# Softmaxes, rotated heads and latents transposed whole in float32 and parted out of PSUM

## The chip, the cores and the metric

The kernel runs on one core of a Trainium2 chip. The metric is the device time of one execution in microseconds; the kernel before takes 2120.96 us (median of 3 runs, 2120.81 to 2120.97). Engine names in the rows are those of the profile: PE is TensorE (PEld its loading of the array), DVE VectorE, ACT ScalarE, SP the queue that issues DMAs.

## The reference

A two-layer encoder over 256 tokens of 2048 features, in float32. Each layer has a token mixer and a channel mixer, each as `x = x + RMSNorm(f(RMSNorm(x)))`:

```
layer 0 mixer: proj = h @ w_in                       # 2048 -> 4608
   A: 8 heads of 128, rotary q and k, dilated windows (as a mask of log counts on full scores)
   B: 8 query heads on 2 key/value heads, RMSNorm of each head's q and k, two-dimensional rotary
   out = [A | B] @ w_out
layer 1 mixer: c = h @ w_in                          # 512 query latents, 512 key/value latents, 64 rotary key
   q = norm(c_q) @ w_uq, k, v = norm(c_kv) @ w_ukv   # 16 heads, 128 + 64 rotary
   out = attention @ w_out
attention: softmax(q k^T * scale) v, 256 x 256 scores for each head
channel mixer: (gelu(conv3(h @ w_gate)) * (h @ w_val)) @ w_down     # 5632 wide
```

## The kernel before, in words

Float32 accuracy comes from splitting: each operand of a product is kept as two float32r tiles, a high part (the value rounded to float32r) and a low part (the value less the high part), and a product is the sum of high times high, high times low and low times high. `parted` (L521) makes them: ScalarE copies the high part, VectorE subtracts it from the value. `parted_by` does it for a value times a row's factor.

Weights stream in chunks of 128 x 1024 (four raw buffers). `_split` parts each, up to two chunks ahead of the products (three buffers of `whi`, `wlo`; L117 on ScalarE, L118 on VectorE). A chunk in `proj_tok` feeds 12 products of 512 columns (L172 to L174), in the channel mixer's `proj_t` 16 products (L186, L187), in layer 1's small projections 24 of 256 columns.

Between chunks, `tick` advances generators by a step each: evacuations of projections (`turned`, `latent`, `evac_qr`, `evac_kr`) and heads (`attend`). The tile framework then orders the instructions of an engine; what is marked to stay in program order (scores and transposes) keeps its place in its own sequence. So attention work lies in between the products of the next projection.

A head in `attend`: scores of two query blocks into one PSUM bank (L471), the maxima on VectorE (L480 or L478), exponentials with row sums on ScalarE (L487) into `p`, the reciprocal (L489). Then `phl`, the two parts of p / sum (L492, L493). Three ticks later each part is turned by four transposes of 128 x 128 (L252, `turn`, against the identity in float32r `ident_r`), eight in all, through two PSUM banks, and ScalarE copies the banks into `pT` (L506). Two ticks later come the products with the values (L172 to L174 `pT,v`) and the parts of the result (L518, L519). `use["phl"]` bounds how many heads hold parts at a time: 1 in layer 0, 2 in layer 1.

`turned` (L538) applies the rotary embedding to up to four heads with the tokens on the partitions (`y`, `z` on VectorE), parts the result into `hl` and turns both parts of each head, four transposes and one ScalarE copy (L574) a head. `latent` in layer 1 does the same for the four 128-wide blocks of a latent (L768). The rotary queries and the shared rotary key of layer 1 (L833, L816) also go through `hl` and `turn`.

PSUM has four banks under the tag `acc` for projections and four under `at` for scores, transposes and attention results. At the seams between sublayers the residual x is transposed in plain float32 against `ident` (L413).

Of the kernel before, what the change touches and what calls it, by code (L numbers as in the profile page):

```python
# [16 lines left out]
P = 128  # L17
T = 256
# [8 lines left out]
HOLD = 3        # chunks of weights kept at the end of an output projection, see proj_tok  # L27
LAGS = 3, 2, 1  # ticks from a softmax to its transposes, from these to the values, from a rotary to its transposes

# columns of the packed vectors  # L30
# [7 lines left out]
class Model:  # L38
    """All products are of operands in two float32r parts, high and low: high high + high low + low high.

    A sublayer's input x is kept as parts of x times the pre-norm's gain, features on the partitions; the norm's
    factor of a token goes in where the products leave PSUM (or into the factors of the scores).
    """
# [14 lines left out]
    def now(self, gen, after=()):  # L58
        """A generator that steps at every tick, once those of `after` have ended."""
        self.soon.append((gen, tuple(after)))  # L60
        return gen

    def later(self, gen, after=()):
        """A generator of the queue, of which a few run at a time."""
        self.bg.append((gen, tuple(after)))
        return gen
# [55 lines left out]
    def behind(self, instructions):  # L122
        """A block whose instructions are issued after these, on their engines."""
        stack = ExitStack()
        for ins in instructions:
            stack.enter_context(self.tc.issue_after(ins.ins))
        return stack

    def weights(self, upto=None):
        """The parts of the next chunk; those after it, before `upto`, get split and loaded."""  # L130
        i = self.at
        if upto is None:
            upto = i + (2 if self.lead else 3)
            self.follow()
        for j in range(i, upto):
            self._split(j)
        for j in range(upto, i + 6):
            self._load(j) if j < upto + 4 else None
        self.at += 1
        return self.made.pop(i)  # L140

    def follow(self):
        """Ahead of a chunk: the tiles of x that it meets, if they aren't there yet."""
# [7 lines left out]
    def warm(self, n):  # L151
        """Products of zeros, for the array's clock to stay up while its next operands get made."""
# [5 lines left out]
    def acc(self, n):  # L158
        """n PSUM banks for sums; evacuations that would still hold them come first."""
# [9 lines left out]
    def mm3(self, ps, lh, ll, rh, rl, start, stop):  # L169
        """ps (+)= l.T @ r of operands in two parts."""  # L170
# [5 lines left out]
    def proj_t(self, nk, x, tag):  # L176
        """[512 outputs] x [256 tokens], outputs on the partitions: 4 PSUM tiles, their halves to be added."""
# [13 lines left out]
    def proj_tok(self, nk, x, order=None, before={}, hold=0):  # L191
        """[256 tokens] x [512 outputs], tokens on the partitions: 2 PSUM tiles.

        The last `hold` chunks are kept for the first half of the tokens to be done before the second.
        """
# [27 lines left out]
    def proj_small(self, x, n, nk):  # L223
        """[256 tokens] x [n outputs] of one chunk of weights [128, nk * n], tokens on the partitions."""
# [12 lines left out]
    def proj_pair(self, x):  # L237
        """Two heads of [128 outputs] x [256 tokens] of one chunk, outputs on the partitions."""
# [11 lines left out]
    def turn(self, out, x):  # L250
        """out[f, t] = x[t, f] of a float32r block."""
        self.tc.keep_in_program_order(self.nc.tensor.transpose(out, x, self.ident_r))  # L252

    def joined(self, sp, out, ps):
        """The sum of a proj_t tile's halves."""
# [9 lines left out]
    def heron(self, s, v, r):  # L265
        """r = 1 / sqrt(v) from the table's root s, by a step of Heron's rule: 2 s / (s s + v)."""
# [6 lines left out]
    def rstd_over(self, ss, r, n, dim):  # L273
        """Factors of a norm of r * x, r a row's factor, from x's square sums ss [128, 2, n], times r."""
# [19 lines left out]
    def table(self, f, x):  # L294
        """Have the table of f loaded ahead of its use, once x [128, 1] is there."""
        self.nc.scalar.activation(self.spare, x, f)

    def pre_norm(self, sp=None):
        """self.r [128 tokens, 2], and on request self.rb [128, 256 tokens] alike on all partitions; a generator."""
# [29 lines left out]
    def split(self, k, src, pre):  # L329
        """Feature tile k of x, transposed, times the gain as two float32r parts."""  # L330
# [11 lines left out]
    def out_proj(self, nk, parts, post, pre, order=None, before={}):  # L342
        """x += post-norm of the output projection; then x's parts for the next product, or x to DRAM.

        The first half of the tokens ends ahead of the second, so that its part of the norm and of the sum lies
        under products; the parts of x come in pairs of feature tiles, of which the next sublayer's first chunks
        of weights ask (see follow).
        """
# [109 lines left out]
    def attend(self, scores, sc, mask, v, v_gen, put, sp):  # L458
        """scores(i): the (lhsT, rhs) of query block i; sc [128 queries, 2]: factors of the scores, or a number;
        v(j): the parts of [128 keys, 128], there once the generator in v_gen has ended; a generator."""  # L460
        nc, use = self.nc, self.use
        while use["phl"] >= self.phl_bufs:
            yield
        use["phl"] += 1
# [8 lines left out]
        p = sp.tile([P, 2, T], F32, tag="p", name="p", bufs=2)  # L473
# [16 lines left out]
        phl = sp.tile([P, 2, 2, T], F32R, tag="phl", name="phl", bufs=self.phl_bufs)  # L490
        for i in range(2):
            nc.scalar.activation(phl[:, 0, i, :], p[:, i, :], AF.Copy, scale=den[:, i:i + 1])  # L492
            nc.vector.scalar_tensor_tensor(out=phl[:, 1, i, :], in0=p[:, i, :], scalar=den[:, i:i + 1],  # L493
                                           in1=phl[:, 0, i, :].bitcast(F32), op0=ALU.mult, op1=ALU.subtract)
# [6 lines left out]
        for a in range(2):  # L501
            pt = self.psum("at", F32R).rearrange("p (j q) -> p j q", j=2)
            for j in range(2):
                for i in range(2):
                    self.turn(pt[:, j, i * P:(i + 1) * P], phl[:, a, i, j * P:(j + 1) * P])
            nc.scalar.copy(pT[:, a], pt.bitcast(F32))  # L506
        use["phl"] -= 1
# [17 lines left out]
    def parted_by(self, hi, lo, x, r):  # L525
        """The parts of x * r."""
# [4 lines left out]
    def mixed(self, sp):  # L531
        """The attention's outputs in parts, feature tiles."""
# [5 lines left out]
    def turned(self, sp, ps, n, block, tab, put, scale=None):  # L538
        """Rotary of n heads, tokens on the partitions, neighbouring blocks of `block` turned against each other,
        times scale(t) of the rows or scale(t, i) of a head's; the parts, transposed, go to put(i); a generator."""  # L540
        nc = self.nc
        parts = []
        for t in range(2):
            x = ps[t][:, :n * P]
            y = sp.tile([P, 512], F32, tag="y", name="y", bufs=1)[:, :n * P]
            z = sp.tile([P, 512], F32, tag="z", name="z", bufs=1)[:, :n * P]
            hl = sp.tile([P, 2, 512], F32R, tag="hl", name="hl", bufs=2)
# [3 lines left out]
            nc.vector.tensor_tensor(out=heads(y), in0=heads(x), in1=tab[:, t, 0].broadcast_to([P, n, P]), op=ALU.mult)  # L551
            for a in range(2):
                nc.vector.tensor_tensor(out=blocks(z)[:, :, :, a, :], in0=blocks(x)[:, :, :, 1 - a, :],
                                        in1=sin[:, :, :, a, :].broadcast_to([P, n, P // block // 2, block]),
                                        op=ALU.mult)
            nc.vector.tensor_tensor(out=y, in0=y, in1=z, op=ALU.add)
            if scale is None:
                self.parted(hl[:, 0, :n * P], hl[:, 1, :n * P], y)
            elif scale.__code__.co_argcount == 1:
                self.parted_by(hl[:, 0, :n * P], hl[:, 1, :n * P], y, scale(t))  # L560
            else:
                for i in range(n):
                    s = slice(i * P, (i + 1) * P)
                    self.parted_by(hl[:, 0, s], hl[:, 1, s], y[:, s], scale(t, i))
            parts.append(hl)
# [3 lines left out]
        for i in range(n):  # L569
            pt = self.psum("at", F32R).rearrange("p (a t) -> p a t", a=2)  # L570
            for a in range(2):
                for t in range(2):
                    self.turn(pt[:, a, t * P:(t + 1) * P], parts[t][:, a, i * P:(i + 1) * P])
            nc.scalar.copy(put(i), pt.bitcast(F32))  # L574
            if i % 2:
                yield

    def first_x(self, sp):
        """The first parts of x, a pair of tiles ahead of each chunk of weights."""
# [24 lines left out]
    def mixer0(self, pre):  # L604
        nc, tc, a = self.nc, self.tc, self.a
        with tc.tile_pool(name="mix0", bufs=1) as sp:
# [7 lines left out]
            self.use, self.phl_bufs = {"phl": 0, "pT": 0}, 1  # L614
# [119 lines left out]
    def mixer1(self, pre):  # L734
        nc, tc, a = self.nc, self.tc, self.a
        with tc.tile_pool(name="mix1", bufs=1) as sp:
# [3 lines left out]
            self.use, self.phl_bufs = {"phl": 0, "pT": 0}, 2  # L740
# [6 lines left out]
            def latent(ps, row, out):  # L747
# [6 lines left out]
                parts = []  # L754
                for t in range(2):
                    y = sp.tile([P, 512], F32, tag="y", name="y", bufs=1)
                    hl = sp.tile([P, 2, 512], F32R, tag="hl", name="hl", bufs=2)
# [258 lines left out]
```

## Time and profile before

| | before |
|---|---|
| median of 3 runs | 2120.96 us |
| profiled execution, span | 2119.2 us |
| TensorE busy | 2106.1 us |
| VectorE busy | 1331.3 us |
| ScalarE busy | 1140.5 us |
| DMA | 385.99 MB, mean 182 GB/s |

The profiled execution's span runs from its first to its last instruction; what lies around it is what is between it and the median of the runs. The two token mixers take 43 to 275 us and 1083 to 1300 us of the span, with the output projections behind them; the channel mixers take most of the rest. A row that groups instructions has their count, their busy time (overlaps counted once), the mean duration of one, and the idle time of the engine just before them with what ended it. In the chain of waits a row is a piece of the path that ended last: start, length, what.

### The profile page before, as it was taken

The numbers are of one execution on the slowest core, as the hardware profiler recorded it, in microseconds if no ns is written. First come the engines' busy times: TensorE is split into PE (matmuls) and PEld (weight loads), VectorE is DVE, ScalarE is ACT, GpSimd is POOL, SyncE is SP. The second block draws the span as 40 slices with busy tenths as digits, with TensorE's granted clock in tenths as the row PEclk, the third lists the DMA queues.
The fourth block names the chain that finished last, engine by engine and source line by source line (L and its number), as shares of the span: only waits on it lengthen the run. The fifth ranks groups of instructions, "written<-read, shape, count | busy, mean of one in ns | idle before, by whom it ended". The sixth has DMA issues, their size and how long they took to land.

```text
span 2119.2 us, 29704 instructions
## 1 busy us (share of the span) xinstructions
PE 2106.1 (99%) x11317; PEld 1787.4 (84%) x11317; DVE 1331.3 (63%) x2004; ACT 1140.5 (54%) x1814; POOL 0.2 (0%) x4
## 2 busy tenths in 40 slices
PE   9999999999999999999999999999999999999998
PEld 7888878888888888888888998788888888888886
DVE  6776657767667666444466764576676766754444
ACT  6766546555555555334355765465555555543433
POOL 0000000000000000000000000000000000000000
PEclk9999999999999999999999999999999999999999
DMA  8545565666666666666655335566666666666664
GB/s 312 170 138 159 167 182 176 182 195 188 191 192 183 195 189 190 191 191 193 194 182 164 102 108 155 169 194 191 190 187 195 184 196 190 185 193 194 194 189 149
DMA packets 108718, 385.99 MB, mean 182 GB/s; under 512 B 12064, under 2 KB 12576, under 8 KB 108576
## 3 DMA queue, kind: packets, MB, share of 16 engines
q1 hardware_dynamic: 108288, 383.83, 60.1%
q8 instruction: 88, 1.44, 0.3%
q14 instruction: 54, 0.44, 0.1%
q10 hardware_dynamic: 288, 0.28, 0.0%
HBM read 381.96 MB, written 2.10 MB: 181 GB/s over the span
## 4 chain that ended last, share of the span: by engine, by line
PE 98%; DVE 1%; ACT 1%; DMA 0%; issue 0%; DVEq 0%; SPq 0%
PE ps L186 31%; PE ps L174 16%; PE ps L172 16%; PE ps L173 16%; PE ps L187 15%; PE ps L471 2%; PE ps L252 2%; DVE x L391 0%; PE ps L413 0%; DMA raw<-in_w_in 0%; ACT whi L117 0%; ACT junk L292 0%; PE ps L789 0%; DVE xhl L528 0%; PE ps L790 0%
## 5 line engine op out<-in xcount | busy, mean ns | idle before, releaser
L118 DVE TENSOR_TENSOR wlo<-raw,whi 128x1024 fp32r<-128x1024 f32 (+1 forms) x710 | 867.1, 1222 | 698.3 <-ACT whi L117 697.6
L117 ACT CAST whi<-raw 128x1024 fp32r<-128x1024 f32 (+1 forms) x710 | 743.8, 1048 | 775.9 <-PE ps L174 421.6
L186 PE MATMUL ps<-xhl,whi 128*128 128x512 f32 x2816 | 978.6, 394 | 1.0 <-DVE xhl L528 1.0
L187 PE MATMUL ps<-xhl,wlo 128*128 128x256 f32 x2816 | 779.1, 277 | 0.0
L186 PEld LDWEIGHTS ps<-xhl,whi 128*128 128x128 f32 x2816 | 527.6, 188 | 123.1 <-DVE xhl L528 2.1
L187 PEld LDWEIGHTS ps<-xhl,wlo 128*128 128x128 f32 x2816 | 528.9, 188 | 1.0 <-DVE wlo L118 0.5
L174 PE MATMUL ps<-whi,gl 128*128 128x512 f32 x704 | 280.9, 399 | 0.0
L173 PE MATMUL ps<-wlo,gh 128*128 128x512 f32 x704 | 277.4, 394 | 0.0
L172 PE MATMUL ps<-whi,gh 128*128 128x512 f32 x704 | 276.0, 392 | 0.0
L173 PEld LDWEIGHTS ps<-wlo,gh 128*128 128x128 f32 x704 | 132.2, 188 | 34.5
L172 PEld LDWEIGHTS ps<-whi,gh 128*128 128x128 f32 x704 | 132.2, 188 | 31.4
L174 PEld LDWEIGHTS ps<-whi,gl 128*128 128x128 f32 x704 | 132.2, 188 | 30.3
L172 PE MATMUL ps<-whi,xhl 128*128 128x512 f32 x352 | 138.5, 395 | 1.5 <-ACT whi L117 1.5
L173 PE MATMUL ps<-wlo,xhl 128*128 128x512 f32 x352 | 137.9, 392 | 0.0
L174 PE MATMUL ps<-whi,xhl 128*128 128x512 f32 x352 | 137.6, 392 | 0.0
L172 PE MATMUL ps<-whi,oh 128*128 128x512 f32 x256 | 101.5, 397 | 0.0
L174 PE MATMUL ps<-whi,ol 128*128 128x512 f32 x256 | 101.4, 396 | 0.0
L173 PE MATMUL ps<-wlo,oh 128*128 128x512 f32 x256 | 100.9, 394 | 0.0
L257 ACT COPY half<-ps 128x256 f32<-128x256 f32 x176 | 65.0, 369 | 45.7 <-PE ps L186 36.0
L172 PEld LDWEIGHTS ps<-whi,xhl 128*128 128x128 f32 x352 | 65.9, 188 | 15.1 <-ACT whi L117 1.7
L174 PEld LDWEIGHTS ps<-whi,xhl 128*128 128x128 f32 x352 | 66.0, 188 | 14.0
L173 PEld LDWEIGHTS ps<-wlo,xhl 128*128 128x128 f32 x352 | 66.1, 188 | 13.3 <-DVE wlo L118 0.9
(177 smaller groups left out, 1722.4 us busy)
## 6 DMA issues: line engine op xcount, KB each, us to landing
raw<-in_w_up SPq DMA_DIRECT2D x352, 512.0 KB, 4.2
raw<-in_w_down SPq DMA_DIRECT2D x176, 512.0 KB, 4.2
raw<-in_w_in SPq DMA_DIRECT2D x88, 512.0 KB, 4.0
raw<-in_w_out SPq DMA_DIRECT2D x64, 512.0 KB, 4.0
gb<-in_post SPq DMA_DIRECT2D x16, 256.0 KB, 4.2
raw<-in_w_qn SPq DMA_DIRECT2D x8, 512.0 KB, 3.6
raw<-in_w_kn SPq DMA_DIRECT2D x8, 512.0 KB, 3.5
raw<-in_w_v SPq DMA_DIRECT2D x8, 512.0 KB, 3.6
```

The lines of the kernel that those rows point to most:

```text
L117: self.nc.scalar.copy(hi[:, s], raw[:, s])
L118: self.nc.vector.tensor_tensor(out=lo[:, s], in0=raw[:, s], in1=hi[:, s].bitcast(F32), op=ALU.subtract)
L172: mm(ps, lh, rh, start=start, stop=False)
L173: mm(ps, lh, rl, start=False, stop=False)
L174: mm(ps, ll, rh, start=False, stop=stop)
L186: mm(out[i], hi[:, s], x(k), start=k == 0, stop=False)
L187: mm(out[i][:, :T], lo[:, s], x(k)[:, :T], start=False, stop=k == nk - 1)
L252: self.tc.keep_in_program_order(self.nc.tensor.transpose(out, x, self.ident_r))
L257: self.nc.scalar.copy(b, ps[:, T:])
L471: nc.tensor.matmul(ps[:, i, :], l, r, start=n == 0, stop=n == len(pairs) - 1))
```

## The change

Softmaxes, rotated heads and latents stay one float32 tile until after the transposes. `turn_whole` turns a float32 block against the float32 identity, half as many transposes, and `parted` makes the two parts from PSUM. The softmax is scaled by its reciprocal in place on VectorE. Two neighbouring heads share a PSUM bank in `turned`, two blocks in `latent`. The row factors that used to come in with the parts are multiplied in ahead (`times`, or a scaling of each head). Heads are now bounded by `p` tiles: 2 in layer 0 (one `phl` before), 4 in layer 1 (two before). The rotary queries and the rotary key of layer 1 are unchanged. The full diff also blanks comments, which moves line numbers: L471 becomes L475, L252 stays for what is unchanged, whole transposes are at L256, the scaling at L495, `parted` at L523 and L524.

```diff
+    def turn_whole(self, out, x):
+        self.tc.keep_in_program_order(self.nc.tensor.transpose(out, x, self.ident))
...
     def attend(self, scores, sc, mask, v, v_gen, put, sp):
-        while use["phl"] >= self.phl_bufs:
+        while use["p"] >= self.p_bufs:
             yield
...
-        phl = sp.tile([P, 2, 2, T], F32R, tag="phl", name="phl", bufs=self.phl_bufs)
         for i in range(2):
-            nc.scalar.activation(phl[:, 0, i, :], p[:, i, :], AF.Copy, scale=den[:, i:i + 1])
-            nc.vector.scalar_tensor_tensor(out=phl[:, 1, i, :], in0=p[:, i, :], scalar=den[:, i:i + 1],
-                                           in1=phl[:, 0, i, :].bitcast(F32), op0=ALU.mult, op1=ALU.subtract)
+            nc.vector.tensor_scalar(out=p[:, i, :], in0=p[:, i, :], scalar1=den[:, i:i + 1], scalar2=None,
+                                    op0=ALU.mult)
...
-        for a in range(2):
-            pt = self.psum("at", F32R).rearrange("p (j q) -> p j q", j=2)
-            for j in range(2):
-                for i in range(2):
-                    self.turn(pt[:, j, i * P:(i + 1) * P], phl[:, a, i, j * P:(j + 1) * P])
-            nc.scalar.copy(pT[:, a], pt.bitcast(F32))
-        use["phl"] -= 1
+        pt = self.psum("at").rearrange("p (j q) -> p j q", j=2)
+        for j in range(2):
+            for i in range(2):
+                self.turn_whole(pt[:, j, i * P:(i + 1) * P], p[:, i, j * P:(j + 1) * P])
+        self.parted(pT[:, 0], pT[:, 1], pt)
+        use["p"] -= 1
...
     def turned(self, sp, ps, n, block, tab, put, scale=None):
-            if scale is None:
-                self.parted(hl[:, 0, :n * P], hl[:, 1, :n * P], y)
-            elif scale.__code__.co_argcount == 1:
-                self.parted_by(hl[:, 0, :n * P], hl[:, 1, :n * P], y, scale(t))
-            else:
+            if scale is not None and scale.__code__.co_argcount == 2:
                 for i in range(n):
                     s = slice(i * P, (i + 1) * P)
-                    self.parted_by(hl[:, 0, s], hl[:, 1, s], y[:, s], scale(t, i))
-            parts.append(hl)
+                    nc.vector.tensor_scalar(out=y[:, s], in0=y[:, s], scalar1=scale(t, i), scalar2=None,
+                                            op0=ALU.mult)
+            whole.append(y)
             yield
...
-        for i in range(n):
-            pt = self.psum("at", F32R).rearrange("p (a t) -> p a t", a=2)
-            for a in range(2):
+        for i in range(0, n, 2):
+            pt = self.psum("at").rearrange("p (i t) -> p i t", i=2)
+            for j in range(2):
                 for t in range(2):
-                    self.turn(pt[:, a, t * P:(t + 1) * P], parts[t][:, a, i * P:(i + 1) * P])
-            nc.scalar.copy(put(i), pt.bitcast(F32))
-            if i % 2:
-                yield
+                    self.turn_whole(pt[:, j, t * P:(t + 1) * P], whole[t][:, (i + j) * P:(i + j + 1) * P])
+            for j in range(2):
+                out = put(i + j)
+                self.parted(out[:, 0, :], out[:, 1, :], pt[:, j, :])
+            yield
...
-            self.use, self.phl_bufs = {"phl": 0, "pT": 0}, 1
+            self.use, self.p_bufs = {"p": 0, "pT": 0}, 2
...
-            self.use, self.phl_bufs = {"phl": 0, "pT": 0}, 2
+            self.use, self.p_bufs = {"p": 0, "pT": 0}, 4
...
             def latent(ps, row, out):
-                for k in range(4):
-                    pt = self.psum("at", F32R).rearrange("p (a t) -> p a t", a=2)
-                    for b in range(2):
+                for k in range(0, 4, 2):
+                    pt = self.psum("at").rearrange("p (i t) -> p i t", i=2)
+                    for j in range(2):
                         for t in range(2):
-                            self.turn(pt[:, b, t * P:(t + 1) * P], parts[t][:, b, k * P:(k + 1) * P])
-                    nc.scalar.copy(out[:, k], pt.bitcast(F32))
+                            self.turn_whole(pt[:, j, t * P:(t + 1) * P], whole[t][:, (k + j) * P:(k + j + 1) * P])
+                    self.parted(out[:, k:k + 2, 0, :], out[:, k:k + 2, 1, :], pt)
```

How this moves instructions shows best at three places. First TensorE in layer 0, where the first softmaxes of the grouped queries are turned under the products of the next projection (`xhl` is a part of the input, `kB` the grouped keys, `q` a head's queries). Before:

```order
L174 MATMUL ps<-whi,xhl_122 128x512
L252 MATMUL ps<-ident_r,phl 128x128 x8
L471 MATMUL ps<-kB,q_648 128x256 x6
L172 MATMUL ps<-whi,xhl_122 128x512
L173 MATMUL ps<-wlo,xhl_122 128x512
L174 MATMUL ps<-whi,xhl_122 128x512
```

Now, at the same chunk:

```order
L174 MATMUL ps<-whi,xhl_122 128x512
L256 MATMUL ps<-ident,p 128x128 x8
L475 MATMUL ps<-kB,q_640 128x256 x6
L475 MATMUL ps<-kB,q_641 128x256 x6
L172 MATMUL ps<-whi,xhl_122 128x512
L173 MATMUL ps<-wlo,xhl_122 128x512
L174 MATMUL ps<-whi,xhl_122 128x512
```

The eight transposes of one head become eight of two heads, and the scores of two further heads follow in place of one's.

Second, TensorE in layer 1, in the middle of the sixteen heads (`cq` the query latents, `qk` a pair's queries and keys, `kr` and `qr` the rotary ones). Before:

```order
L174 MATMUL ps<-whi,cq 128x256
L252 MATMUL ps<-ident_r,phl 128x128 x16
L172 MATMUL ps<-cq,whi 128x256
L173 MATMUL ps<-cq,whi 128x256
L471 MATMUL ps<-qk 128x256 x3
L471 MATMUL ps<-kr,qr 128x256 x2
```

Now:

```order
L174 MATMUL ps<-whi,cq 128x256
L256 MATMUL ps<-ident,p 128x128 x8
L475 MATMUL ps<-qk 128x256 x3
L475 MATMUL ps<-kr,qr 128x256 x2
L475 MATMUL ps<-qk 128x256 x3
L475 MATMUL ps<-kr,qr 128x256 x2
```

Sixteen transposes of a pair of heads become eight; the two products that stood between them and the next scores come later.

Third, VectorE in layer 0 while the second projection of grouped queries is evacuated (`wlo` a low part of weights, `nm` the maxima, `y` and `z` the rotary work). Before:

```order
L118 TENSOR_TENSOR wlo<-raw,whi 128x1024
L523 TENSOR_TENSOR hl<-y,hl 128x512
L480 TENSOR_REDUCE nm<-ps 128x2
L118 TENSOR_TENSOR wlo<-raw,whi 128x1024
L484 TENSOR_TENSOR nm<-nm,rr 128x2
L118 TENSOR_TENSOR wlo<-raw,whi 128x1024
L489 RECIPROCAL den<-den 128x2
L118 TENSOR_TENSOR wlo<-raw,whi 128x1024
L493 SCALAR_TENSOR_TENSOR phl<-p,den,phl 128x256 x2
```

Now:

```order
L118 TENSOR_TENSOR wlo<-raw,whi 128x1024
L524 TENSOR_TENSOR pT<-ps,pT 128x512 x2
L484 TENSOR_REDUCE nm<-ps 128x2 x2
L488 TENSOR_TENSOR nm<-nm,rr 128x2
L285 TENSOR_SCALAR v_939<-hs,r_938 128x4
L488 TENSOR_TENSOR nm<-nm,rr 128x2
L563 TENSOR_TENSOR y<-y,z 128x512
L118 TENSOR_TENSOR wlo<-raw,whi 128x1024
L493 RECIPROCAL den<-den 128x2
L557 TENSOR_TENSOR y<-ps,tabB_144 128x512
L495 TENSOR_SCALAR p<-p,den 128x256 x2
```

The work of two heads and the low parts out of PSUM now stand between two splits of weights, where one head's was spread over several.

## Rows read from the trace of the kernel before

**Rows 1.** The page's first part: busy time, share of the span, instructions.
```profile
PE 2106.1 (99%) x11317; PEld 1787.4 (84%) x11317; DVE 1331.3 (63%) x2004; ACT 1140.5 (54%) x1814; POOL 0.2 (0%) x4
```

**Rows 2.** Waits of PE and PEld: total us, times, longest.
```profile
PE ps L172 <- ACT whi L117: 1.5, 1, 1.5
PE ps L413 <- DVE x L391: 1.1, 3, 0.4
PE ps L156 <- DVE zeros L928: 1.1, 1, 1.1
PE ps L186 <- DVE xhl L528: 1.0, 2, 0.5
...
PEld ps L173 <- DVE wlo L118: 0.9, 2, 0.4
PEld ps L252 <- ACT hl L522: 0.8, 3, 0.3
```

**Rows 3.** Costliest groups of the page: the splits of weights.
```profile
L118 DVE TENSOR_TENSOR wlo<-raw,whi 128x1024 fp32r<-128x1024 f32 (+1 forms) x710 | 867.1, 1222 | 698.3 <-ACT whi L117 697.6
L117 ACT CAST whi<-raw 128x1024 fp32r<-128x1024 f32 (+1 forms) x710 | 743.8, 1048 | 775.9 <-PE ps L174 421.6
```

**Rows 4.** The chain of waits over the whole span, by line.
```profile
by line: PE ps L186 30.8%; PE ps L174 16.0%; PE ps L172 15.9%; PE ps L173 15.8%; PE ps L187 15.3%; PE ps L471 2.1%; PE ps L252 1.6%; DVE x L391 0.3%; PE ps L413 0.3%; DMA raw<-in_w_in 0.2%; ACT whi L117 0.2%; ACT junk L292 0.2%; issue 0.2%;
```

**Rows 5.** Both mixers as stretches: us, then PE, PEld, DVE, ACT, POOL, clock.
```profile
43.00:275.00 232.00, 231.80 (x1242) 194.56 (x1241) 161.19 (x282) 155.52 (x307) 0.00 (x0) 1.00 0.53 159
1083.00:1300.00 217.00, 216.49 (x1474) 191.56 (x1473) 145.17 (x259) 145.25 (x296) 0.00 (x0) 1.00 0.46 136
```

**Rows 6.** Groups by line and shape: transposes on PE.
```profile
L252 PE MATMUL ps<-ident_r,phl 128*128 128x128 f32 x256 | 25.8, 244 | 0.0
L252 PE MATMUL ps<-ident_r,hl 128*128 128x128 f32 x172 | 18.4, 245 | 0.2
L413 PE MATMUL ps<-ident,x 128*128 128x128 f32 x96 | 16.0, 275 | 1.2 <-DVE x L391 1.1
```

**Rows 7.** Chain in layer 0's mixer: a head's transposes, scores, one value product of six.
```profile
122.80 0.64 PE ps L252 x8
123.44 0.78 PE ps L471 x6
...
130.07 0.12 PE ps L172
```

**Rows 8.** Chain at the start of layer 0's channel mixer.
```profile
356.25 0.12 PE ps L187
356.38 0.44 PE ps L413 x4
356.81 0.23 PE ps L186
```

**Rows 9.** Chain at the start of layer 1's mixer.
```profile
1100.54 0.44 PE ps L413 x4
```

**Rows 10.** Groups by line and shape: ACT in softmax and attention.
```profile
L506 ACT CAST pT<-ps 128x512 fp32r<-128x512 f32 x64 | 33.8, 592 | 1.4 <-PE ps L252 1.4
L492 ACT ACTIVATE phl<-p,den 128x256 fp32r<-128x256 f32 x64 | 28.9, 504 | 1.2 <-DVE den L489 1.1
...
L518 ACT CAST oh<-ps 128x256 fp32r<-128x256 f32 x32 | 11.6, 371 | 2.7 <-PE ps L174 2.2
```

**Rows 11.** Groups by line and shape: DVE in softmax and attention.
```profile
L493 DVE SCALAR_TENSOR_TENSOR phl<-p,den,phl 128x256 fp32r<-128x256 f32 x64 | 28.0, 480 | 7.0 <-ACT phl L492 7.0
...
L519 DVE TENSOR_TENSOR ol<-ps,oh 128x256 fp32r<-128x256 f32 x32 | 13.0, 418 | 4.1 <-ACT oh L518 4.1
...
L523 DVE TENSOR_TENSOR qk<-ps,qk 128x512 fp32r<-128x512 f32 x16 | 10.9, 684 | 1.3 <-ACT qk L522 1.2
...
L482 DVE TENSOR_SCALAR nm<-nm 128x2 f32<-128x2 f32 x16 | 2.6, 162 | 0.1
```

More of the change, by code (lines that the diff above doesn't have):

```diff
@@ L461, in attend @@
         nc, use = self.nc, self.use
-        while use["phl"] >= self.phl_bufs:
+        while use["p"] >= self.p_bufs:
             yield
-        use["phl"] += 1
+        use["p"] += 1
         num = isinstance(sc, float)
@@ L472, in attend @@
         nm, den = self.col("nm", 2, 3), self.col("den", 2, 3)
-        p = sp.tile([P, 2, T], F32, tag="p", name="p", bufs=2)
+        p = sp.tile([P, 2, T], F32, tag="p", name="p", bufs=self.p_bufs)
         if mask is not None:
@@ L541, in turned @@
         nc = self.nc
-        parts = []
+        whole = []
         for t in range(2):
             x = ps[t][:, :n * P]
-            y = sp.tile([P, 512], F32, tag="y", name="y", bufs=1)[:, :n * P]
+            y = sp.tile([P, 512], F32, tag="y", name="y", bufs=4)[:, :n * P]
             z = sp.tile([P, 512], F32, tag="z", name="z", bufs=1)[:, :n * P]
-            hl = sp.tile([P, 2, 512], F32R, tag="hl", name="hl", bufs=2)
             heads = lambda a: a.rearrange("p (h f) -> p h f", f=P)
@@ L550, in turned, with times @@
             sin = tab[:, t, 1].rearrange("p o (n s b) -> p o n s b", s=2, b=block)
-            nc.vector.tensor_tensor(out=heads(y), in0=heads(x), in1=tab[:, t, 0].broadcast_to([P, n, P]), op=ALU.mult)
+            def times(out, a, b):
+                if scale is not None and scale.__code__.co_argcount == 1:
+                    nc.vector.scalar_tensor_tensor(out=out, in0=a, scalar=scale(t), in1=b,
+                                                   op0=ALU.mult, op1=ALU.mult)
+                else:
+                    nc.vector.tensor_tensor(out=out, in0=a, in1=b, op=ALU.mult)
+            times(heads(y), heads(x), tab[:, t, 0].broadcast_to([P, n, P]))
             for a in range(2):
-                nc.vector.tensor_tensor(out=blocks(z)[:, :, :, a, :], in0=blocks(x)[:, :, :, 1 - a, :],
-                                        in1=sin[:, :, :, a, :].broadcast_to([P, n, P // block // 2, block]),
-                                        op=ALU.mult)
+                times(blocks(z)[:, :, :, a, :], blocks(x)[:, :, :, 1 - a, :],
+                      sin[:, :, :, a, :].broadcast_to([P, n, P // block // 2, block]))
             nc.vector.tensor_tensor(out=y, in0=y, in1=z, op=ALU.add)
-            if scale is None:
-                self.parted(hl[:, 0, :n * P], hl[:, 1, :n * P], y)
-            elif scale.__code__.co_argcount == 1:
-                self.parted_by(hl[:, 0, :n * P], hl[:, 1, :n * P], y, scale(t))
-            else:
+            if scale is not None and scale.__code__.co_argcount == 2:
                 for i in range(n):
                     s = slice(i * P, (i + 1) * P)
-                    self.parted_by(hl[:, 0, s], hl[:, 1, s], y[:, s], scale(t, i))
-            parts.append(hl)
+                    nc.vector.tensor_scalar(out=y[:, s], in0=y[:, s], scalar1=scale(t, i), scalar2=None,
+                                            op0=ALU.mult)
+            whole.append(y)
             yield
@@ L753, in latent @@
                 rr = self.rstd_over(ss, self.r, 1, 512)
-                parts = []
+                whole = []
                 for t in range(2):
-                    y = sp.tile([P, 512], F32, tag="y", name="y", bufs=1)
-                    hl = sp.tile([P, 2, 512], F32R, tag="hl", name="hl", bufs=2)
+                    y = sp.tile([P, 512], F32, tag="y", name="y", bufs=2)
                     nc.vector.scalar_tensor_tensor(out=y, in0=ps[t], scalar=rr[:, t, :], in1=g,
                                                    op0=ALU.mult, op1=ALU.mult)
-                    self.parted(hl[:, 0, :], hl[:, 1, :], y)
-                    parts.append(hl)
+                    whole.append(y)
                 yield
-                for k in range(4):
-                    pt = self.psum("at", F32R).rearrange("p (a t) -> p a t", a=2)
-                    for b in range(2):
+                for k in range(0, 4, 2):
+                    pt = self.psum("at").rearrange("p (i t) -> p i t", i=2)
+                    for j in range(2):
                         for t in range(2):
-                            self.turn(pt[:, b, t * P:(t + 1) * P], parts[t][:, b, k * P:(k + 1) * P])
-                    nc.scalar.copy(out[:, k], pt.bitcast(F32))
+                            self.turn_whole(pt[:, j, t * P:(t + 1) * P], whole[t][:, (k + j) * P:(k + j + 1) * P])
+                    self.parted(out[:, k:k + 2, 0, :], out[:, k:k + 2, 1, :], pt)
             def rope(y, z, v, n):
@@ L779, in room @@
             def room(tag, n):
-                t = sp.tile([P, 512], F32, tag=tag, name=tag, bufs=1)
+                t = sp.tile([P, 512], F32, tag=tag, name=tag, bufs=2 if tag == "y" else 1)
                 return t[:, :2 * n * 64].rearrange("p (t h f) -> p t h f", t=2, f=64)
@@ L796, in evac_kr @@
                 k, y, z = (room(tag, 1) for tag in ("grow", "y", "z"))
-                raw = sp.tile([P, 512], F32, tag="p", name="raw", bufs=2)[:64]
+                raw = sp.tile([P, 512], F32, tag="p", name="raw", bufs=self.p_bufs)[:64]
                 nc.scalar.copy(raw[:, T:], ps[:64, T:])
```

## The prediction

> **What bounds the kernel now.** I read the page's first part first, then the waits of TensorE, then the chain of waits, and last the stretches of the two token mixers. TensorE is busy for 2106.1 of 2119.2 us [rows 1]. A busy engine may still be paced by another one, so the waits come next: over the whole program TensorE's products wait 4.7 us in seven places, for the first weights, the first zeros and the residual between sublayers, and its loads of the array 0.9 us for low parts of weights and 0.8 us for `hl` [rows 2]. ScalarE's split of the weights (L117), in turn, sits idle for 775 us, and what ends that is nearly always TensorE [rows 3]. So the splits wait for the products, not the products for the splits. The chain that ended last says the same: its shares of TensorE add up to 98%, and 1.6%, some 34 us, is line L252, the transposes that the change halves [rows 4]. In the two mixers (43 to 275 us and 1083 to 1300 us) TensorE is busy in 448.3 of 449 us at the full granted clock, VectorE in 306.4 and ScalarE in 300.8, both stretches added [rows 5]. Whatever TensorE no longer has to do there comes off the end, as long as the other two engines stay ahead.
>
> **What the transposes cost on the path.** The trace has 256 transposes of softmax parts and 172 of `hl` parts, 428 in all [rows 6]. The change keeps those of the shared rotary key (4) and of the rotary queries (4 times 8): 36. The other 392 become 196: 128 of softmaxes (4 for each of 32 heads), 52 of rotated heads (2 for each of 26), 16 of latents. The duration of one matmul (244 ns) overlaps with the next, so I take the step on the chain. Eight float32r transposes take 0.64 us of it, and the six products behind them 0.78 us, where six products of that size elsewhere take 6 x 0.12 = 0.72 us [rows 7]: together 0.70 us for a group of eight.
>
> The new transposes are whole float32 blocks against the plain identity. That kind is in the trace already: L413 turns the residual x in the same way, 96 times [rows 6]. In the middle of dense products, four of them take 0.44 us, with the product before and the one behind at their usual 0.12 and 0.23 us [rows 8]; in the next sublayer's first products, which are of the mixers' kind, it is again 0.44 us [rows 9]. So 0.11 us each, against 0.088 us for the old kind: one whole transpose is a quarter dearer, but stands for two.
>
> 392 / 8 = 49 groups. Before: 49 x 0.70 = 34.3 us. After: 49 x 0.44 = 21.6 us. The difference, 12.7 us, lies wholly on the path. Bounds: by the busy time of the rows, which counts the scattered transposes and their tails, it is 392 x (25.8 + 18.4) / 428 = 40.5 us before [rows 6]. Against 196 x 0.11 that saves 18.9 us; against 196 x 16.0 / 96 = 32.7 us, the mean busy time of L413 that includes its waits at the sublayers' seams, 7.8 us. I take 12.7 and add 0.5 of the 0.8 us that L252 waits for `hl` [rows 2], since a cast and a subtraction ahead of the transposes go: 13.2 us.
>
> A rule of the Trainium skill speaks against this: "FP8 and Floating Point Precision", section TensorE Precision Notes, says that true float32 goes through the array in four passes. The trace disagrees for a transpose [rows 8, 9]; what four passes would make of the sum is the third rival below.
>
> **What moves on the other engines.** *Softmax, 32 heads.* ScalarE loses two scaled copies of 0.504 us and one of two copies of 0.592 us out of PSUM [rows 10]: 1.60 us a head, 51 us in all. VectorE loses two subtractions of 0.480 us [rows 11] and gains one subtraction 512 wide out of PSUM at 0.684 us (the row of `qk`, same operands) and two scalings 256 wide in place. No row has such a scaling: from below it is bounded by the fixed part, 0.162 us for 2 elements, from above by 0.480 us, the form with a third operand; I take 0.418 us, a two-operand pass of that width [rows 11]. That makes 1.52 us for 0.96: +0.56 us a head, +18 us in all (+2 to +22). *Rotated heads.* Four heads had six copies 512 wide (0.592 us) on ScalarE and two subtractions of 0.684 us on VectorE; now there are four copies of 0.371 us and four subtractions of 0.418 us, out of PSUM [rows 10, 11]: ScalarE -2.1 us, VectorE +0.3 us for each of the six projections, which I round to +3 us in all for the scaling of the keys, now done before the turn. *Latents.* ScalarE has two such copies for six, -2.4 us each, VectorE as much as before.
>
> VectorE thus goes from 306 to about 327 us of 449, minus the 13 saved: 75%; ScalarE falls to about 232. All of it lies beside the products, so I cost it at nothing. The cover is this: the splits run two chunks ahead, and a chunk is 12 products at 0.23 us [rows 8], so VectorE may fall behind by some 5.5 us before a product waits for its low part. If the cover is gone, TensorE stands for whatever is over.
>
> **What the order moves.** In layer 0 one head could hold its parts at a time, now two softmaxes may be held, so heads pass in pairs: eight transposes, then the scores of two heads. In layer 1 heads were in pairs before; sixteen transposes become eight in the same place, and the scores follow them at once, where two products had been put between, since only two of four PSUM banks are taken now. No DMA is moved: weights come in the same order, and the load queue is asked by the same steps.
>
> The subtraction of the low part stands behind the transposes now, so the values wait for a copy and a subtraction (0.59 + 0.68 us) instead of two copies (1.18 us). Queued behind that wait on TensorE are the products of the values, two ticks later, that is 24 products or more: over 5 us away, so nothing is late by 0.1 us.
>
> **Sum.** 2119.2 - 13.2 = 2106.0 us for the span. The median of the runs, 2120.96, is 1.8 us above the profiled span [rows 1]; that part is the same afterwards: 2107.8 us, 0.62% faster.
>
> **Rivals.** *VectorE is late in layer 0's bursts.* With two heads in one tick VectorE has two maxima and two subtractions 512 wide (0.68 us each), four passes over two elements (0.16) and four scalings (0.42) [rows 11] between two splits: 5.1 us, and 6.3 with a split of 1.22 us [rows 3], against 5.5 us of cover; one head had 2.0. At 0.8 us late for each of 8 pairs it gives back 6.4 us: 2114 us. For it: VectorE is busy in 161 of 232 us in layer 0 and waits in order. Against it: the same ticks hold on TensorE 0.88 us of transposes and 12 products of 0.12 us for the scores beside the chunk, layer 1 ran pairs all along, and a wait for low parts came to 0.9 us in the whole run [rows 2].
>
> *Nothing changes.* If TensorE's step were set by something that arrives (DMA or split), transposes would be filling time that is empty anyway: 2121 us. For it: a full TensorE looks like that too, as matmul ends are modelled. Against it: steps of 0.23 and 0.12 us repeat without spread, and L117 is released by products [rows 3].
>
> *Whole transposes cost four passes.* Then the kernel is slower. A 256-column product takes 0.12 us, so 128 columns take 0.06 us a pass and four passes 0.24 us: 196 x 0.24 = 47.0 us against 34.3 us, +12.7 us, 2133.7 us. It decides from 0.175 us for one (34.3 / 196). The four-pass rule named above would bring this about. Against it: L413 takes 0.11 us wherever it stands among products [rows 8, 9]; for it only that these 96 stand in few places.
>
> **How the numbers follow.** Forecast 0.82, late VectorE 0.11, no change 0.04, four passes 0.03. The forecast's own range is 2103 to 2112: the saving of 18.9 us less a little, to the saving of 7.8 us and something. For 8 in 10 I stretch it to 2103 to 2113, into the late VectorE. Within 0.2% (4.2 us, about what a measurement here can tell from no change) counts as the same: the forecast and nearly all of the second case are faster, 0.92; same 0.05; slower 0.03.
>
> **What would show it.** In the new profile: a group of whole transposes for softmax and rotated heads, 196 in number, with four at 0.44 us on the chain; 196 fewer matmuls; TensorE's busy time down to about 2093 us with waits as few as before; ScalarE's busy time down by 68 us or so, VectorE's up by about 20. A first step wrong would be L256 above 0.15 us each; a second, waits of TensorE for `wlo` (L118) in 60 to 250 us that come to several us; a third, that the span falls by much less than the busy time of transposes.

## The result and the profile after

| | before | after |
|---|---|---|
| median of 4 runs each | 2120.97 us | 2104.69 us (2104.64 to 2104.93) |
| profiled execution, span | 2119.2 us | 2102.9 us |
| mixer 0, first product to first transpose of x | 332.57 us | 322.92 us |
| mixer 1, between two such seams | 287.22 us | 280.40 us |
| the two channel mixers together | 1484.0 us | 1484.4 us |

The ratio of after to before is 0.990, 95% interval 0.9869 to 0.9931. The changed kernel is 16.3 us faster; 13.2 us were forecast. In some runs of most kernels here, the one before among them (2130.13 us), one or both of the channel mixers take 751 instead of 742 us whatever the edit, at a granted clock of 0.998 to 0.999 either way and for a cause that wasn't looked for, so times below are of runs without that, and traces are compared by their token mixers alone. The token mixers hold all of the gain: 9.65 and 6.82 us (the stages are cut at TensorE's first product and at the first transpose of x of each seam).

The page's first part, after (busy time, share of the span, instructions):

```profile
PE 2090.2 (99%) x11121; PEld 1775.0 (84%) x11121; DVE 1342.3 (64%) x2050; ACT 1081.8 (51%) x1694; POOL 0.2 (0%) x4
```

Against [rows 1], TensorE has 196 matmuls fewer and 15.9 us less to do, nearly the whole gain of the span: it was busy before and is busy now. ScalarE lost 58.7 us and VectorE gained 11.0, and neither shows in the time.

TensorE's waits after, then those of its loads of the array (us in total, times, longest):

```profile
PE ps L417 <- DVE x L395: 1.4, 3, 0.7
PE ps L156 <- DVE zeros L931: 1.1, 1, 1.1
PE ps L172 <- ACT whi L117: 1.0, 1, 1.0
PE ps L186 <- DVE xhl L529: 1.0, 2, 0.5
...
PEld ps L173 <- DVE wlo L118: 0.9, 2, 0.4
...
PEld ps L256 <- DVE y L567: 0.3, 1, 0.3
```

These are the waits of [rows 2] again: the first weights, the first zeros, the residual between sublayers. The wait for low parts of weights (`wlo`), by which a late VectorE would be seen, is 0.9 us as before. The 0.8 us for `hl` are gone, and 0.3 us for the rotated `y` stand instead. More waits of before are not in the list any more. Two are of the scores' loads for copies by ScalarE, three of the transposes' loads, for further parts of `hl` and for a softmax part; the forecast had looked at none of these five:

```profile
PEld ps L471 <- ACT pT L506: 0.7, 3, 0.3
PEld ps L471 <- ACT q L574: 0.7, 2, 0.4
...
PEld ps L252 <- ACT hl L527: 0.5, 1, 0.5
PEld ps L252 <- DVE hl L523: 0.5, 2, 0.3
...
PEld ps L252 <- ACT phl L492: 0.3, 1, 0.3
```

They are short, but they lie on the path: a load that comes late makes the step of its transpose or product longer. Taken from the trace, each such step in the token mixers less what the same step takes elsewhere, they add up to 3.1 us before: 1.55 at the transposes, 1.6 at the loads of scores and value products (waits of the splits and of the seams left out). After, 0.4 us are left.

The two stretches of the mixers after (columns as in [rows 5]):

```profile
43.00:275.00 232.00, 232.00 (x1166) 195.20 (x1166) 172.24 (x318) 127.74 (x250) 0.00 (x0) 1.00 0.55 166
1083.00:1300.00 217.00, 216.96 (x1414) 192.03 (x1413) 149.67 (x266) 118.68 (x231) 0.00 (x0) 1.00 0.47 142
```

TensorE is busy in 448.96 of 449 us at the full granted clock, VectorE in 321.9 (the prediction had about 327), ScalarE in 246.4 (about 232). The fuller VectorE is still a quarter idle.

The turned groups by line and shape (count, then busy us and mean ns of one), to be set against [rows 6]:

```profile
L256 PE MATMUL ps<-ident,p 128*128 128x128 f32 x128 | 16.6, 272 | 0.0
L256 PE MATMUL ps<-ident,y 128*128 128x128 f32 x68 | 10.2, 272 | 0.0
L252 PE MATMUL ps<-ident_r,hl 128*128 128x128 f32 x36 | 3.8, 243 | 0.0
```

128 + 68 = 196 whole transposes, and 36 of the old kind are left, as counted. And their places on the chain of waits in layer 0's mixer (start, length, what):

```profile
54.07 0.33 PE ps L256 x3
54.40 0.23 PE ps L172
...
97.46 0.44 PE ps L256 x4
...
111.75 0.87 PE ps L256 x8
112.62 1.43 PE ps L475 x12
```

Three, four or eight whole transposes take 0.11 us each, and the product behind them its usual 0.23; two heads pass as a pair, eight transposes and twelve scores. The old kind was less even. On the same chain of before, at the first rotated heads:

```profile
56.95 0.13 PE ps L252 x2
57.08 0.30 PE ps L173
57.38 0.38 PE ps L252 x5
57.76 0.30 PE ps L174
```

Two old transposes took 0.13 us by their own step, but the product behind them 0.30 instead of 0.23: a piece has a tail of 0.07 us. Its first two transposes are shorter for it, 0.06 us each by these rows, so a broken piece is little dearer: with the tail, 0.11 us for a single one, 0.10 us each for two, 0.09 for five, 0.088 for eight [rows 7] and 0.086 for sixteen:

```profile
1185.41 1.31 PE ps L252 x16
1186.72 0.19 PE ps L172
```

What makes old pieces dearer is a wait. Here two, eight and eight of them take 0.24, 0.74 and 0.87 us where 0.13 and 0.64 are usual, each with a load that came late, for `hl`, `phl` and `hl`:

```profile
1117.82 0.24 PE ps L252 x2
262.93 0.74 PE ps L252 x8
1158.59 0.87 PE ps L252 x8
```

From both traces, each piece with what the two products behind it take above their usual: the 428 old transposes cost 39.5 us in 56 pieces, of which 1.55 us are the waits above and 38.0 steps and tails. The 36 that stay take 3.3 us of that, so the other 392 took 34.7 us, 0.0885 each. The 196 whole ones take 21.4 us, 0.109 each in pieces of any size. So steps and tails gave 34.7 - 21.4 = 13.3 us, the waits 3.1 - 0.4 = 2.7 us, and 0.25 us lie ahead of the first product: 16.25 us, where the runs gave 16.3.

### The profile page after: what moved, and what is told of

It reads as the page before. It is cut to its first block, busy times and chain, and to the rows that moved or that the text cites. A ratio compares the mean times of both kernels' runs of the same rounds, so it can differ in the third digit from the quotient of the medians.

```text
span 2102.9 us, 29245 instructions
## 1 busy us (share of the span) xinstructions
PE 2090.2 (99%) x11121; PEld 1775.0 (84%) x11121; DVE 1342.3 (64%) x2050; ACT 1081.8 (51%) x1694; POOL 0.2 (0%) x4
## 4 chain that ended last, share of the span: by engine, by line
PE 99%; DVE 1%; DMA 0%; ACT 0%; issue 0%; DVEq 0%; SPq 0%
PE ps L186 31%; PE ps L174 16%; PE ps L172 16%; PE ps L173 16%; PE ps L187 15%; PE ps L475 2%; PE ps L256 1%; DVE x L395 0%; PE ps L417 0%; DMA raw<-in_w_in 0%; PE ps L792 0%; PE ps L252 0%; ACT junk L296 0%; DVE xhl L529 0%; PE ps L793 0%
```

## The experiments

Two theories of the 3.1 us beyond the forecast were put on record with the runs. *A*: the step of a transpose was the cause and the old ones were dearer than forecast, since broken groups each pay the tail; what the pairs of heads in layer 0 bring is small. *B*: the transposes gave what was forecast, and the pairs gave the rest. Neither has the waits as a cause of their own: A's prices of an old transpose (0.0917 us, 23.2 us for the softmaxes, 12.75 for `hl`) contain those at the transposes. What each run's trace shows of the waits is said with it. The prediction's own rivals are tried as well. Times below are medians; before ran beside each at 2121.0 us.

**The softmaxes alone.** Before, with the change of `attend` and its bounds only:

```diff
-                    self.turn(pt[:, j, i * P:(i + 1) * P], phl[:, a, i, j * P:(j + 1) * P])
...
+                self.turn_whole(pt[:, j, i * P:(i + 1) * P], p[:, i, j * P:(j + 1) * P])
```

> The kernel before with the softmax part of the change alone (whole p, two and four p tiles); rotated heads and latents as before. Theory A (the price of the turned groups in the trace: 23.2 us of softmax parts become 14.0 us): 2120.97 - 9.2 = 2111.7 us, down to 2110.7 if the short waits beside the softmaxes go too. Theory B (about 3 us of the gain come from heads passing in pairs, the rest from counts at 0.70 and 0.44 us a group): 32 x 0.26 = 8.3 us and 3 us, 2109.7 us.

2110.33 us (ratio 0.9943, 0.9923 to 0.9962): 10.7 us saved, 5.3 in each mixer. That is between the two theories' numbers. By steps and tails, 256 transposes of softmax parts cost 22.7 us and 128 whole ones 14.0: 8.7 us. The waits of its trace come to 1.5 us on the path, 1.7 less than before, which makes 10.4: the scores' waits for `pT` and those for `phl` are gone, the ones for `hl` stay, and one of two for `q`:

```profile
PEld ps L252 <- ACT hl L522: 0.8, 3, 0.3
...
PEld ps L474 <- ACT q L574: 0.4, 1, 0.4
```

Since layer 1 had its pairs already and still saved as much as layer 0, pairs can't be the bulk.

**The rotated heads and latents alone.** After, with `attend` and its bounds as before, and one `hl` buffer in layer 1, for room:

```diff
-                self.turn_whole(pt[:, j, i * P:(i + 1) * P], p[:, i, j * P:(j + 1) * P])
...
+                    self.turn(pt[:, j, i * P:(i + 1) * P], phl[:, a, i, j * P:(j + 1) * P])
...
-                hl = sp.tile([P, 2, 512], F32R, tag="hl", name="hl", bufs=2)
+                hl = sp.tile([P, 2, 512], F32R, tag="hl", name="hl", bufs=1)
```

> The change for rotated heads and latents alone; the softmax as before, one or two heads' parts held (in layer 1 hl has one buffer for two, for room). Theory A: 12.75 us of hl groups become 7.5 us: 2120.97 - 5.3 = 2115.7 us. Theory B: 17 groups at 0.26 us, nothing from pairs: 2116.6 us. If both halves together with the other run fall short of 16.3 us, the halves help each other.

2115.4 us (0.9979, 0.9962 to 0.9997): 5.6 us saved, nearer to A's number. Steps and tails make 4.6 us of it (136 transposes at 0.0885 against 68 at 0.109). Here the waits for `hl` at the turned heads are gone and the scores' waits for `pT` stay, 1.0 us less on the path than before:

```profile
PEld ps L475 <- ACT pT L510: 0.9, 4, 0.3
```

With the run above 10.7 + 5.6 = 16.3 us: the two parts of the change add up to the whole, so neither hides behind the other.

**One softmax at a time in layer 0, two in layer 1.** After, with half the softmaxes held:

```diff
-            self.use, self.p_bufs = {"p": 0, "pT": 0}, 2
+            self.use, self.p_bufs = {"p": 0, "pT": 0}, 1
...
-            self.use, self.p_bufs = {"p": 0, "pT": 0}, 4
+            self.use, self.p_bufs = {"p": 0, "pT": 0}, 2
```

> The changed kernel with as few softmaxes held as before: one p tile in layer 0, two in layer 1, so that heads pass one by one in layer 0. Theory A (the price of turned groups): no change beyond 0.7 us, 2104.7 to 2105.4 us. Theory B (pairs): the 3 us beyond the forecast go again, 2107.7 us or more.

2105.36 and 2105.53 us, the two of six runs that can be compared (the other four took 2114.3 to 2114.6, the profiled one among them). In the trace mixer 0 is 1.0 us longer than after and mixer 1 is the same. A head's piece of the chain:

```profile
77.92 0.44 PE ps L256 x4
78.35 0.72 PE ps L475 x6
```

The pair is undone (four and six in place of eight and twelve) and costs nothing on these rows. What it costs are new waits of the value products' loads for `pT`, 0.6 us on the path:

```profile
PEld ps L172 <- ACT pT L523: 0.5, 2, 0.3
...
PEld ps L172 <- DVE pT L524: 0.4, 1, 0.4
```

B needed 2107.7 or more and falls. The pairs are worth 0.7 to 1.0 us.

**The old number of transposes, as plain float32.** Before, with its 392 part transposes against the plain identity:

```diff
+    def turn_f32(self, out, x):
+        self.tc.keep_in_program_order(self.nc.tensor.transpose(out.bitcast(F32), x.bitcast(F32), self.ident))
...
-                    self.turn(pt[:, j, i * P:(i + 1) * P], phl[:, a, i, j * P:(j + 1) * P])
+                    self.turn_f32(pt[:, j, i * P:(i + 1) * P], phl[:, a, i, j * P:(j + 1) * P])
```

Rotated heads and latents have the same edit.

> The kernel before with the same 392 transposes of parts (softmaxes, rotated heads, latents), but as plain float32 against the plain identity; counts, parts and order as before. Theory A (0.109 us for a whole one anywhere, 0.0917 us for a float32r one, pieces and tails counted): 392 x 0.0175 = +6.8 us, 2127.8 us. By the forecast's terms (0.11 against 0.0875): +8.6 us, 2129.6 us. Four passes (0.24 us): +58 us.

2128.5 us, 7.5 us above before (ratio 1.0016, 0.999 to 1.0042, an interval that by itself doesn't exclude no change). The mixers of the traces say the same: 337.09 - 332.57 and 290.28 - 287.22, 7.6 us. The chain at a head:

```profile
79.90 0.87 PE ps L255 x8
80.78 0.71 PE ps L474 x6
```

Eight now take 0.87 instead of 0.64 us, and the six scores behind them 0.71 instead of 0.78 [rows 7]. So the tail belongs to the float32r kind alone. The measured 7.5 lies between A's 6.8 and the 8.6 of the forecast's own terms, far from the 58 of four passes. By steps and tails, 392 x (0.1093 - 0.0885) = 8.2 us come on top; the waits of this trace are 0.5 us shorter than before, which leaves 7.7.

**Each whole transpose twice.** After, the same output written twice:

```diff
     def turn_whole(self, out, x):
-        self.tc.keep_in_program_order(self.nc.tensor.transpose(out, x, self.ident))
+        for _ in range(2):
+            self.tc.keep_in_program_order(self.nc.tensor.transpose(out, x, self.ident))
```

> The changed kernel with each of the 196 whole transposes issued twice into the same place. If transposes lie wholly on the path: 196 x 0.109 = +21.4 us, 2126.1 us. If something else paces TensorE, less than half of that. Four passes: +47 us.

2126.02 us (1.0003 of before, 0.9978 to 1.0027): 21.3 us above after for 196 more transposes, 0.109 us each. Mixer 0 grew by 12.73 us for its 116 and mixer 1 by 8.74 for its 80: 0.110 and 0.109.

```profile
124.69 0.87 PE ps L257 x8
125.56 0.12 PE ps L172
```

Eight for one head take 0.87 us, and the product behind comes at 0.12. Every transpose is on the path in full, so "nothing changes", in which transposes fill empty time, is out; a price of four passes is out too.

**More work for VectorE.** After, with three further passes of 512 columns a head ahead of the scalings, into a tile that nobody reads:

```diff
+        for _ in range(3):
+            idle = self.small.tile([P, 512], F32, tag="idle", name="idle", bufs=1)
+            flat = p.rearrange("p i k -> p (i k)")
+            nc.vector.tensor_tensor(out=idle, in0=flat, in1=flat, op=ALU.mult)
```

> The changed kernel with three more VectorE passes of 512 columns for each head (3 x 0.68 = 2.05 us a head, 66 us in all; their output is not used). By the rival of late VectorE (5.5 us of cover behind a pair of heads): each pair in layer 0 adds 4.1 us to 6.3, 4.9 us late, eight times: +39 us, 2144 us. By the slack of the stretches (VectorE busy 172 of 232 us in layer 0, 150 of 217 us in layer 1): 33 us fit into either: within 3 us of 2104.7 us.

2110.14 to 2111.73 us in the five of ten runs that can be compared: 5.4 to 7.0 us above after (ratio to before 0.995, 0.9921 to 0.9978). The added work by line, and the new waits of TensorE and of its loads:

```profile
L497 DVE TENSOR_TENSOR idle<-p 128x512 f32<-128x512 f32 x96 | 65.3, 680 | 0.1
```

```profile
PE ps L256 <- DVE p L499: 2.5, 1, 2.5
PE ps L174 <- DVE wlo L118: 1.1, 1, 1.1
...
PEld ps L174 <- DVE wlo L118: 1.3, 1, 1.3
```

65 us more of VectorE, 2.0 us a head and 4.1 a pair, cost about 6 us (3.8 and 1.8 in the two mixers of the trace). Two single waits hold most of that, not one at every pair: a transpose in layer 0 waits for its scaled softmax, and a product in layer 1 for low parts of weights (the last two rows are that one wait, seen at the product and at its load). Neither number on record was met: VectorE is far from "late at each pair" (39 us), and its slack isn't endless either (more than 3). With VectorE busy in 376 of the 449 us of the two stretches there are such waits; after, at 322, there are none.

**The low rotary product over all 128 rows.** The chain of after has an odd row in layer 1's mixer, the scores of two heads, and the product behind them:

```profile
1176.98 3.73 PE ps L475 x20
1180.71 0.32 PE ps L172
```

Twenty products of 256 columns take 3.73 us where 0.12 each would be 2.4. Four of them use 64 rows of the array. After, with the full height (this adds low times low to the score):

```diff
-  (qr[0][:, h % 4, bs], kr[:, 0, :]), (qr[0][0:64, h % 4, bs], kr[0:64, 1, :])]
+  (qr[0][:, h % 4, bs], kr[:, 0, :]), (qr[0][:, h % 4, bs], kr[:, 1, :])]
```

> The changed kernel with the low-part rotary score product over all 128 rows (kr holds the low keys on both halves, so low times low is added) in place of 64 rows. In the trace 32 such products of 64 rows step by 0.31 us, those of 128 rows by 0.117 us. If the half-height array load is what costs, 32 x 0.19 = 6.2 us go: 2098.5 us. If the step comes from the place (the change of bank at the end of a block), nothing changes: 2104.7 us.

2092.23 us, 12.5 us below after and 28.8 below before (0.9885 of before, 0.9836 to 0.9934): twice the larger number expected, and faster than both kernels. Mixer 1 alone moved, from 280.40 to 267.76 us. The same place on the chain:

```profile
1174.03 2.35 PE ps L475 x20
...
1176.49 0.12 PE ps L173
```

In after's trace, from start to start, a 64-row product takes 0.31 us, the product ahead of it 0.21 and the one behind 0.22; with all rows each takes 0.118. That is 0.39 us for each of 32, 12.5 us. The expectation had priced the step of its own alone, not its neighbours'. Why a lower product costs this isn't shown; that its height is the cause is, since nothing else was changed. By line and shape after, then with all rows:

```profile
L475 PE MATMUL ps<-kr,qr 64*128 64x256 f32 x32 | 12.2, 382 | 0.0
L475 PE MATMUL ps<-kr,qr 128*128 128x256 f32 x32 | 9.0, 282 | 0.0
```

```profile
L475 PE MATMUL ps<-kr,qr 128*128 128x256 f32 x64 | 12.8, 281 | 0.0
```

Sixty-four products of full height take 12.8 us busy, where thirty-two of them and thirty-two half ones took 21.2.

## Where the prediction held, and which of its terms was off

**The path.** "Whatever TensorE no longer has to do there comes off the end" held, in both directions: 15.9 us less busy time gave 16.3 us, and doubling the transposes gave back exactly their steps.

**The new price.** 0.44 us for four, read from transposes of another tile in another stage [rows 8, 9], was right: 0.109 us each in pieces of three, four and eight, over 196 of them and over 196 more, 21.4 us where 21.6 was taken. The Trainium skill, "FP8 and Floating Point Precision", section TensorE Precision Notes, has float32 in four passes. The runs disagree for a transpose against the identity: 0.109 us, where four passes would have been 0.24 us by the forecast's estimate.

**The old price.** The step was "together 0.70 us for a group of eight". Applied to all 392 transposes as 49 x 0.70 = 34.3 us, it held as well: 34.7 us by steps and tails. That the rotated heads are broken into ones, twos and fives between products costs little. The bound by busy time, 40.5 us before, was too high: its rows count durations (0.24 us, against steps of 0.06 to 0.09) that overlap with the products around each piece. Steps and tails gave 13.3 us for the forecast 12.7.

**The term that failed: the waits.** The forecast took "0.5 of the 0.8 us that L252 waits for `hl`". It measured 2.7 us, and that is most of the 3.1 us by which the sum fell short. [rows 2] stop after the first line of L252's waits; further down the same list of before stand the five lines shown with the result. The transposes no longer wait for a part of `hl` or `phl`, which gave 1.4 us, and scores and value products hardly wait for copies any more, which gave 1.3. The forecast saw the second place ("since only two of four PSUM banks are taken now") and gave it no price. The same two terms, steps with tails at 0.0885 and 0.109 us a transpose and the waits read from each trace, give every other run that moved transposes or heads (us, against before or after):

| | steps and tails | waits | sum | token mixers measured |
|---|---|---|---|---|
| the change, against before | -13.3 | -2.7 | -16.0 | -16.5 |
| softmaxes alone, against before | -8.7 | -1.7 | -10.4 | -10.5 |
| heads and latents alone, against before | -4.6 | -1.0 | -5.6 | -5.5 |
| one softmax at a time, against after | 0 | +0.7 | +0.7 | +1.0 |
| old number as float32, against before | +8.2 | -0.5 | +7.7 | +7.6 |
| each whole one twice, against after | +21.4 | 0 | +21.4 | +21.5 |

(The token mixers gained 16.5 us, the channel mixers lost 0.4 of it.) What is left, up to 0.5 us, isn't placed, nor are the 0.25 us ahead of the first product, where the change does nothing. The prices per transpose come from the traces of before and after themselves; the other rows test them.

**The other engines.** The scaling had no row of its own. 64 of them have 19.7 us busy, 0.31 each, where 0.418 was taken:

```profile
L495 DVE TENSOR_SCALAR p<-p,den 128x256 f32<-128x256 f32 x64 | 19.7, 350 | 0.9
L524 DVE TENSOR_TENSOR pT<-ps,pT 128x512 fp32r<-128x512 f32 x32 | 20.6, 682 | 0.0
```

That is 7 of the 9 us by which VectorE grew less than the forecast 20. ScalarE fell by 58.7, not 68. More than half of that is because counts were multiplied by mean durations, which overlap between neighbours:

```profile
L523 ACT CAST pT<-ps 128x512 fp32r<-128x512 f32 x32 | 17.2, 585 | 0.0
```

With the 33.8 and 28.9 us busy of [rows 10], the softmaxes lost 33.8 + 28.9 - 17.2 = 45.5 us, not 51. Both slips were on covered engines and cost the forecast nothing.

**The rivals.** Late VectorE: no new wait for `wlo` after, and 65 us more of it cost 6, of which 1.1 in one wait for `wlo`. The rival had 6.3 us in one burst against 5.5 us of cover, and the added passes made that 10.4; whether its burst was put too long or its cover too short isn't shown. (In the order shown with the change, the scalings come behind the next split, not in one burst with the rest.) Nothing changes, and four passes: both refuted by the doubled transposes.

## What to carry to other kernels

Where TensorE is dense, price a matmul by its step on the chain together with the product behind it, and then read the whole list of waits of the array's loads: waits of 0.2 to 0.5 us that are single lines there, and that a change takes away with their cause, were 2.7 of 16.3 us here. Turning a value whole before it is split halves the transposes, and at 0.109 against 2 x 0.0885 us each that is a gain wherever the engines that then split it have room. And read the chain for rows that are longer than their count times the usual step: one such row, in lines that the change didn't touch, was worth 12.5 us, three quarters of what the change itself brought.

## What the runs showed of the hardware that was not expected

- A product over 64 rows among products over 128 rows takes 0.31 us for 256 columns instead of 0.118, and slows the product ahead of it and the one behind by 0.09 and 0.10 us (32 of them: 12.5 us).
- A float32r transpose steps faster than a float32 one (0.64 against 0.87 us for eight) but leaves 0.07 us on the product behind its piece; the float32 one leaves nothing.
- Loads of the array that come 0.2 to 0.5 us late lengthen TensorE's path although it is busy in 99% of the span: 3.1 us before, 0.4 after.
